# Output projection with seven k-tiles held, and the MLP's first two blocks split by token tile

## The chip, the core and the metric

The kernel runs on one core of one Trainium2 chip. The metric is the device time of one execution in microseconds (us): the median of three runs of the kernel before is 450.49 us (450.48 to 450.57). Names of engines: PE is TensorE's matmul, PEld its weight load, DVE is VectorE, ACT is ScalarE, POOL is GpSimd, SP is SyncE, which issues the loads here.

## What is computed

One layer of a hybrid decoder on 256 tokens of 1024 features, in float32. A token mixer of three gated branches (a short convolution, block-sparse attention, cross-attention into 256 memory tokens) gives `merged`; then

```
x = x + rmsnorm(merged @ w_out, g_post_mix)          # output projection, norm, residual
h = rmsnorm(x, g_pre_ffn)                            # second norm
u = causal_dwconv(h @ w_up, ffn_conv_w, ffn_conv_b)  # 1024 -> 2 x 2816, width 3 over tokens
a, g = split(u)
f = (gelu(a) * g) @ w_down                           # 2816 -> 1024
x = x + rmsnorm(f, g_post_ffn)
```

A norm needs the mean square of a whole row of 1024 features, so nothing of a token's row can be scaled before the last of its columns is there. The change lies in the first three of these lines.

## The kernel before

**Precision.** Each float32 operand is split into two parts, high and low (`hilo`, L265 to L269, for activations; `split_until`, L216 on ACT for `wh` and L217 on DVE for `wl`, for weights), and a product is three matmuls: high by high, high by low, low by high. Where a block of 128 output features is made for all 256 tokens (`mm_wide`, L242 and L244), eight matmuls of 512 columns take both parts of the activations at once and eight of 256 columns add the weights' low parts; ACT and DVE then add the two halves up (L249, L250).

**Weights.** They come from HBM in one stream, in the order of their use: loads of 1 MB, each of two pieces of 128x1024, into three `raw` buffers (L191, issued by SP). A piece is split into a pair from a pool of five (`PARTS`), or into a place lent by a tile that is no longer needed (`extra`): before the change three pieces of w_up go into the places `A`, `A` and `E`. A load can start when DVE has split the earlier content of its buffer; a split into the pool can start when PE has finished with the piece five places back. `weights()` hands the next piece out and splits `ahead` pieces more; with `hold` the piece handed out before is not given back yet.

**Output projection.** Tokens are two tiles of 128 (t = 0 and 1); the 1024 features that are summed over are eight k-tiles. `po[t]` is a pair of PSUM banks of 512 columns each. `down_tile` (L256) runs a k-tile for a token tile as six matmuls of 512 columns: three products by two banks. The first three k-tiles run for both tiles; the last five are held, so that tile 0 can be ended first (its last two k-tiles bank by bank) while tile 1 still has work. The loop is in the hands of a scheduler, which puts the instructions of each engine in an order by its own estimates; pieces of tile 1 can so come between those of tile 0.

**Norms and the second tile** (`residual`, written as a fixed order). `post_norm` takes the mean square on ACT (L279, one instruction for each bank), the factor on three small POOL instructions (L282 to L284), the gain and the residual on DVE (L664, L667). For tile 0 a second mean square follows, and `xs` (L706) is the scaled row. PE turns `xs` into columns (`turn`, L312, eight 128x128 transposes into `tp`). Tile 1's matmuls run meanwhile. Then tile 1's norm, eight transposes of its unscaled `x1`, and ACT (L714) and DVE (L716) make the two parts of `h2T`, eight pieces of 128x256 that hold both tiles. The factor of tile 1's second norm is applied later, after the up projection.

**MLP, first blocks.** `both_blocks` runs the first two blocks of 128 features of w_up side by side: 32 matmuls of 256 columns on the high part of `h2T` (L374, L375), then 16 on its low part (L378). From then on blocks follow one another (`mm_wide`) to the end, with the down projection (`pf`, L256) between them.

Of the kernel before, what the change touches and what calls it, by code (L numbers as in the profile page):

```python
# [12 lines left out]
F32R = mybir.dt.float32r  # L13
BF16 = mybir.dt.bfloat16
AF = mybir.ActivationFunctionType
ALU = mybir.AluOpType
# [84 lines left out]
def trunk(ctx, tc, x, mem, memT_in, weights_in, par_in, rel_bias, g_post_mix, g_post_ffn, buckets, out):  # L101
# [11 lines left out]
    def f32(ap):  # L113
        return ap.bitcast(F32)
# [44 lines left out]
    used, freed = 0, 0  # L159
    extra = dict(zip(range(first_up, first_up + 3), ("A", "A", "E")))  # L160
    extra_tiles = {}
# [3 lines left out]
    def part_tiles(i):  # L165
        if i not in extra:
            return [wp.tile([P, 1024], F32R, tag=tag, name=tag, bufs=PARTS) for tag in ("wh", "wl")]
        tag = extra[i]
        if tag not in extra_tiles:
            extra_tiles[tag] = [sb.tile([P, 2 if tag == "E" else 4, 1024], F32R, tag=tag, name="wx"), 0]  # L170
        t, n = extra_tiles[tag]
        extra_tiles[tag][1] += 2
        return [t[:, n], t[:, n + 1]]
# [193 lines left out]

    def both_blocks(a):

        ws = [weights(hold=i > 0) for i in range(2)]  # L370
        d = acc("ft")
        for k in range(KT):
            for i, (wh, wl) in enumerate(ws):
                nc.tensor.matmul(d[i][:, :S], wh[:, k], a[:, 0, k], start=(k == 0), stop=False)  # L374
                nc.tensor.matmul(d[i][:, :S], wl[:, k], a[:, 0, k], start=False, stop=False)  # L375
        for i, (wh, _) in enumerate(ws):
            for k in range(KT):
                nc.tensor.matmul(d[i][:, S:], wh[:, k], a[:, 1, k], start=False, stop=(k == KT - 1))  # L378
        return d

# [301 lines left out]

    for k in range(KT):
        w = weights(hold=k > KT - 5)
        if k < KT - 5:
            for t in range(NT):
                down_tile(po[t], [parts_of(mg, k, k, t, w)], KT)
        else:
            held.append((k, w))
            if k < KT - 2:  # L690
                down_tile(po[0], [parts_of(mg, k, k, 0, w)], KT)
    down_tile(po[0], [parts_of(mg, k, k, 0, w) for k, w in held[3:]], KT, True)
    split_until(first_up + 3)
    x1 = sb.tile([P, NT, D], F32, tag="qm", name="x1")
    h2T = parts_tile(KT, "B", "h2T")
    r2, dg2, r2s = [], [], []

    def residual():
        post_norm(po[0], x_sb[:, 0], gains[:, 0], x1[:, 0], "ro")
        r2.append(rstd_full(x1[:, 0], "r2"))  # L700
        down_tile(po[1], [parts_of(mg, k, k, 1, w) for k, w in held[:3]], KT)
        down_tile(po[1], [parts_of(mg, k, k, 1, w) for k, w in held[3:]], KT, True)
        banks = [bank("tp") for _ in range(KT // 2)]
        tps = [two(banks[k // 2])[:, k % 2] for k in range(KT)]
        xs = wk.tile([P, 1, D], F32, tag="pT", name="xs", bufs=2)
        nc.vector.tensor_scalar_mul(xs[:, 0], x1[:, 0], r2[0])  # L706
        for k in range(KT):
            turn(tps[k], xs, 0, k)
        post_norm(po[1], x_sb[:, 1], gains[:, 0], x1[:, 1], "ro", (0, 256, 512, D))
        for k in range(KT):  # L710
            turn(tps[k], x1, 1, k)
        for k in range(0, KT, 2):
            for j in (k, k + 1):
                nc.scalar.activation(h2T[:, 0, j], tps[j], AF.Copy, scale=gf[:, j:j + 1])  # L714
            for j in (k, k + 1):
                nc.vector.scalar_tensor_tensor(h2T[:, 1, j], tps[j], gf[:, j:j + 1], f32(h2T[:, 0, j]), op0=ALU.mult,  # L716
                                               op1=ALU.subtract)
        r2.append(rstd_full(x1[:, 1], "r2"))
# [5 lines left out]
    def up(c, f, b0):  # L724
# [23 lines left out]
        for half in (1, 0):  # L748
            u = wk.tile([P, 2 * S], F32, tag="y", name="u", bufs=YB)[:, :n * S]
            res.append(u)  # L750
            if c == 0 and half:
                late.append((half, u, both_blocks(h2T)))
                continue
# [99 lines left out]
```

## Time and profile before

| what | before |
| --- | --- |
| median of three runs | 450.49 us |
| the profiled execution, own time | 449.86 us |
| its span, first to last instruction | 448.1 us |
| PE busy, share of the span | 97% |
| DVE, ACT busy | 80%, 65% |
| output projection on PE | 231.9 to 254.0 us |
| first two MLP blocks on PE | 257.8 to 263.6 us |
| DMA queues, mean | 186 GB/s |

The profile is of one execution; its own time is 0.63 us under the median. Times below are us from the start of its span. The list of instructions in order of time shows, for each engine, when an instruction started, how long it took, and in brackets how long the engine had been idle before it and what ended that. Matmuls are pipelined: one that takes 0.39 us is followed by the next 0.23 us after it started, so a row "x6" has its first start and the end of its sixth.

### The profile page before, as it was taken

To read this page: it belongs to the slowest core of one execution; us is meant where nothing else is said; L and a number is where in the kernel's file an instruction comes from. 1 tells how busy PE (TensorE), PEld (TensorE's weight loads), DVE (VectorE), ACT (ScalarE), POOL (GpSimd) and SP (SyncE) were. 2 spreads that over 40 slices of the span, in tenths; PEclk is the share of its full clock that TensorE was granted. 3 is DMA by queue.
4 is the path that set the end of the run, shared out by engine and by line. 5 is a ranking of instruction groups with operands and counts; after the bars stand their busy time and mean duration, and the time that the engine had idled before them with its cause. 6 is when DMAs were issued, how large, how long until landed. Compare 5 with 4: busy or idle time off the path is not lost.

```text
span 448.1 us, 6694 instructions
## 1 busy us (share of the span) xinstructions
PE 435.7 (97%) x2425; PEld 375.7 (84%) x2425; DVE 358.2 (80%) x635; ACT 292.4 (65%) x533; POOL 15.6 (3%) x40
## 2 busy tenths in 40 slices
PE   7999999999999999999999899999999999999993
PEld 4797888888888998888888698888888888888882
DVE  4687789969987788698777579997878878788875
ACT  5984776756687776675655468866657657657642
POOL 0212000000000000000000300000000000000001
PEclk9999999999999999999999999999999999999998
DMA  7994765534535443555767036555556546546102
GB/s 241 411 407 178 245 225 187 187 114 171 187 105 190 176 144 140 187 177 195 249 225 279 5 140 236 189 187 191 193 182 198 189 176 203 189 176 209 70 1 94
DMA packets 14828, 83.45 MB, mean 186 GB/s; under 512 B 1827, under 2 KB 2636, under 8 KB 6092
## 3 DMA queue, kind: packets, MB, share of 16 engines
q1 hardware_dynamic: 14060, 80.92, 50.9%
q10 hardware_dynamic: 432, 1.05, 0.8%
q0 software_dynamic: 304, 1.06, 0.7%
q8 instruction: 19, 0.31, 0.3%
q14 instruction: 13, 0.11, 0.1%
HBM read 81.96 MB, written 1.06 MB: 185 GB/s over the span
## 4 chain that ended last, share of the span: by engine, by line
PE 91%; ACT 2%; DVE 1%; issue 1%; POOL 0%; POOLq 0%; DVEq 0%; ACTq 0%
PE ft L242 42%; PE ft L244 21%; PE pf L256 13%; PE po L256 5%; PE pv L256 2%; PE po L261 1%; ACT wh L216 1%; ACT junk L279 1%; PE at L261 1%; PE tp L312 0%; PE ft L233 0%; PE ft L378 0%; PE ft L234 0%; PE ft L374 0%; PE ft L235 0%
## 5 line engine op out<-in xcount | busy, mean ns | idle before, releaser
L216 ACT ACTIVATE wh<-raw 128x1024 fp32r<-128x1024 f32 (+1 forms) x139 | 143.1, 1033 | 104.3 <-PE ft L242 66.8
L217 DVE TENSOR_TENSOR wl<-raw,wh 128x1024 fp32r<-128x1024 f32 (+1 forms) x139 | 165.2, 1192 | 55.6 <-ACT wh L216 53.0
L242 PE MATMUL ft<-hT,wh 128*128 128x512 f32 x384 | 97.2, 393 | 0.0
L242 PE MATMUL ft<-h2T,wh 128*128 128x512 f32 x328 | 82.2, 392 | 0.0
L242 PEld LDWEIGHTS ft<-hT,wh 128*128 128x128 f32 x384 | 69.0, 189 | 12.2
L242 PEld LDWEIGHTS ft<-h2T,wh 128*128 128x128 f32 x328 | 59.5, 189 | 11.0
L244 PEld LDWEIGHTS ft<-hT,wl 128*128 128x128 f32 x384 | 52.2, 190 | 3.6
L244 PE MATMUL ft<-hT,wl 128*128 128x256 f32 x384 | 53.6, 282 | 0.0
L249 ACT ACTIVATE t<-ft 128x256 f32<-128x256 f32 x116 | 43.0, 372 | 10.4 <-PE ft L244 10.3
L256 PE MATMUL pf<-wh,f 128*128 128x512 f32 x176 | 49.2, 390 | 0.0
L244 PEld LDWEIGHTS ft<-h2T,wl 128*128 128x128 f32 x328 | 44.9, 190 | 3.3
L244 PE MATMUL ft<-h2T,wl 128*128 128x256 f32 x328 | 45.9, 282 | 0.0
L256 PEld LDWEIGHTS pf<-wh,f 128*128 128x128 f32 x176 | 32.4, 188 | 6.2
L250 DVE TENSOR_TENSOR y<-ft,t 128x256 f32<-128x256 f32 x68 | 28.2, 418 | 2.9 <-ACT t L249 2.6
L256 PE MATMUL pf<-wl,f 128*128 128x512 f32 x88 | 27.5, 390 | 0.0
L745 ACT ACTIVATE u<-v,par 128x256 f32<-128x256 f32 x44 | 24.0, 589 | 3.8 <-DVE v L739 3.7
L594 DVE SCALAR_TENSOR_TENSOR u<-v,par,u 128x255 f32<-128x255 f32 x44 | 19.7, 477 | 0.7 <-ACT u L745 0.7
L595 DVE SCALAR_TENSOR_TENSOR u<-v,par,u 128x254 f32<-128x254 f32 x44 | 19.6, 476 | 0.1
L256 PEld LDWEIGHTS pf<-wl,f 128*128 128x128 f32 x88 | 16.5, 188 | 3.5
L250 DVE TENSOR_TENSOR v<-ft,t 128x256 f32<-128x256 f32 x44 | 17.9, 417 | 0.5 <-ACT t L249 0.5
L256 PE MATMUL po<-wh,mg 128*128 128x512 f32 x64 | 17.9, 389 | 0.0
L282 POOL TENSOR_SCALAR se<-ss 128x1 f32<-128x1 f32 x10 | 3.4, 344 | 404.7 <-ACT junk L279 404.6
(172 smaller groups left out, 549.3 us busy)
## 6 DMA issues: line engine op xcount, KB each, us to landing
raw<-in_weights_dram SPq DMA_DIRECT2D x66, 1024.0 KB, 4.8
raw<-in_weights_dram SPq DMA_DIRECT2D x8, 256.0 KB, 5.7
rawx<-in_weights_dram SPq DMA_DIRECT2D x4, 512.0 KB, 10.2
rawx<-in_weights_dram SPq DMA_DIRECT2D x2, 1024.0 KB, 9.7
raw<-in_weights_dram SPq DMA_DIRECT2D x2, 512.0 KB, 6.9
m_sb<-in_mem_dram SPq DMA_DIRECT2D x2, 512.0 KB, 7.4
x_sb<-in_x_dram SPq DMA_DIRECT2D x2, 512.0 KB, 9.6
bias<-bd POOLq DMA_DIRECT2D x1, 1024.0 KB, 6.1
```

The lines of the kernel that those rows point to most:

```text
L216: nc.scalar.activation(hi, v, AF.Copy)
L217: nc.vector.tensor_tensor(lo, v, f32(hi), ALU.subtract)
L242: nc.tensor.matmul(p, wh[:, k], a[:, :, k], start=(k == 0), stop=False)
L244: nc.tensor.matmul(p[:, :S], wl[:, k], a[:, 0, k], start=False, stop=(k == kt - 1))
L249: nc.scalar.activation(t, p[:, S:], AF.Copy)
L250: nc.vector.tensor_tensor(dst, p[:, :S], t, ALU.add)
L256: nc.tensor.matmul(d, a, w[:, c:c + 512], start=(first and w is wh and a is ah), stop=(last and a is al))
L261: nc.tensor.matmul(dst, a[i], b[j], start=(first and n == 0), stop=(last and n == 2))
L279: nc.scalar.activation(junk, src, AF.Square, scale=D ** -0.5, accum_out=q)
L594: nc.vector.scalar_tensor_tensor(t[:, 1:], src[:, :S - 1], w1, t[:, 1:], op0=ALU.mult, op1=ALU.add)
L595: nc.vector.scalar_tensor_tensor(t[:, 2:], src[:, :S - 2], w0, t[:, 2:], op0=ALU.mult, op1=ALU.add)
L745: nc.scalar.activation(d, v[:, i], AF.Identity, bias=bb, scale=w2)
```

## The change

Four things.

1. Of the output projection's eight k-tiles seven are held (k = 1 to 7) in place of five, and only k = 0 runs for both tiles in the loop. The two last k-tiles' weights get places of their own (`G` and `mk`), and w_up gets a fourth one (`bias`), so six pieces of weights are now in lent places. The loop is written inside a fixed order for PE; `residual` has such an order too, and between the two the scheduler still places the instructions.
2. In `residual`, tile 1's k-tiles 1 to 5 stand ahead of tile 0's transposes and its k-tiles 6 and 7 behind them, bank by bank.
3. The parts of `h2T` are made tile by tile (`spread_out`): sixteen pieces of 128x128 on each of ACT and DVE in place of eight of 128x256.
4. `both_blocks` is gone. `wide_of` runs the first two blocks for one token tile: for each k-tile and block one matmul that takes the high and the low part side by side (2x128 columns), 16 for a tile. Tile 0's stand behind tile 1's last k-tiles and ahead of tile 1's transposes, tile 1's behind its `h2T`. `low_of` then adds the weights' low parts for both tiles (16 matmuls of 256 columns).

The number of matmul columns is the same: 48 matmuls of 256 columns for the two blocks, 96 of 512 for the projection.

```diff
--- before.py
+++ after.py
@@ -157,7 +157,7 @@
     RAWS, PARTS, AHEAD = 3, 5, 3
     raws, parts = [], []
     used, freed = 0, 0
-    extra = dict(zip(range(first_up, first_up + 3), ("A", "A", "E")))
+    extra = dict(zip(range(first_up - 2, first_up + 4), ("G", "mk", "A", "A", "E", "bias")))
     extra_tiles = {}
     lent = {3: ("C", 0), 4: ("C", 1), 5: ("qm", 0), 6: ("cT", 0)}
     lent_tiles = {}
@@ -167,7 +167,7 @@
             return [wp.tile([P, 1024], F32R, tag=tag, name=tag, bufs=PARTS) for tag in ("wh", "wl")]
         tag = extra[i]
         if tag not in extra_tiles:
-            extra_tiles[tag] = [sb.tile([P, 2 if tag == "E" else 4, 1024], F32R, tag=tag, name="wx"), 0]
+            extra_tiles[tag] = [sb.tile([P, 4 if tag == "A" else 2, 1024], F32R, tag=tag, name="wx"), 0]
         t, n = extra_tiles[tag]
         extra_tiles[tag][1] += 2
         return [t[:, n], t[:, n + 1]]
@@ -365,18 +365,17 @@
                 evac(b - 1, y)
             yield
 
-    def both_blocks(a):
-
-        ws = [weights(hold=i > 0) for i in range(2)]
-        d = acc("ft")
+    def wide_of(d, ws, a, t):
+
         for k in range(KT):
-            for i, (wh, wl) in enumerate(ws):
-                nc.tensor.matmul(d[i][:, :S], wh[:, k], a[:, 0, k], start=(k == 0), stop=False)
-                nc.tensor.matmul(d[i][:, :S], wl[:, k], a[:, 0, k], start=False, stop=False)
-        for i, (wh, _) in enumerate(ws):
+            for p, (wh, _) in zip(d, ws):
+                nc.tensor.matmul(two(p)[:, :, tok(t)], wh[:, k], a[:, :, k, tok(t)], start=(t == 0 and k == 0),
+                                 stop=False)
+
+    def low_of(d, ws, a):
+        for p, (_, wl) in zip(d, ws):
             for k in range(KT):
-                nc.tensor.matmul(d[i][:, S:], wh[:, k], a[:, 1, k], start=False, stop=(k == KT - 1))
-        return d
+                nc.tensor.matmul(p[:, :S], wl[:, k], a[:, 0, k], start=False, stop=(k == KT - 1))
 
     def run(gen):
         for _ in gen:
@@ -680,41 +679,51 @@
     def parts_of(a, k, j, t, w):
         return (k, a[:, 0, j, tok(t)], a[:, 1, j, tok(t)], w[0][:, 0], w[1][:, 0])
 
-    for k in range(KT):
-        w = weights(hold=k > KT - 5)
-        if k < KT - 5:
-            for t in range(NT):
-                down_tile(po[t], [parts_of(mg, k, k, t, w)], KT)
-        else:
-            held.append((k, w))
-            if k < KT - 2:
-                down_tile(po[0], [parts_of(mg, k, k, 0, w)], KT)
-    down_tile(po[0], [parts_of(mg, k, k, 0, w) for k, w in held[3:]], KT, True)
-    split_until(first_up + 3)
+    with tc.manual_schedule(engines={mybir.EngineType.PE}):
+        for k in range(KT):
+            w = weights(hold=k > 1)
+            if k < 1:
+                for t in range(NT):
+                    down_tile(po[t], [parts_of(mg, k, k, t, w)], KT)
+            else:
+                held.append((k, w))
+                if k < KT - 2:
+                    down_tile(po[0], [parts_of(mg, k, k, 0, w)], KT)
+        down_tile(po[0], [parts_of(mg, k, k, 0, w) for k, w in held[-2:]], KT, True)
+    split_until(first_up + 4)
     x1 = sb.tile([P, NT, D], F32, tag="qm", name="x1")
     h2T = parts_tile(KT, "B", "h2T")
-    r2, dg2, r2s = [], [], []
+    r2, dg2, r2s, first = [], [], [], []
 
     def residual():
         post_norm(po[0], x_sb[:, 0], gains[:, 0], x1[:, 0], "ro")
         r2.append(rstd_full(x1[:, 0], "r2"))
-        down_tile(po[1], [parts_of(mg, k, k, 1, w) for k, w in held[:3]], KT)
-        down_tile(po[1], [parts_of(mg, k, k, 1, w) for k, w in held[3:]], KT, True)
+        down_tile(po[1], [parts_of(mg, k, k, 1, w) for k, w in held[:-2]], KT)
         banks = [bank("tp") for _ in range(KT // 2)]
         tps = [two(banks[k // 2])[:, k % 2] for k in range(KT)]
         xs = wk.tile([P, 1, D], F32, tag="pT", name="xs", bufs=2)
         nc.vector.tensor_scalar_mul(xs[:, 0], x1[:, 0], r2[0])
-        for k in range(KT):
-            turn(tps[k], xs, 0, k)
+
+        def spread_out(src, t):
+            for k in range(KT):
+                turn(tps[k], src, t, k)
+            for k in range(0, KT, 2):
+                for j in (k, k + 1):
+                    nc.scalar.activation(h2T[:, 0, j, tok(t)], tps[j][:, tok(t)], AF.Copy, scale=gf[:, j:j + 1])
+                for j in (k, k + 1):
+                    nc.vector.scalar_tensor_tensor(h2T[:, 1, j, tok(t)], tps[j][:, tok(t)], gf[:, j:j + 1],
+                                                   f32(h2T[:, 0, j, tok(t)]), op0=ALU.mult, op1=ALU.subtract)
+
+        spread_out(xs, 0)
+        down_tile(po[1], [parts_of(mg, k, k, 1, w) for k, w in held[-2:]], KT, True)
+        ws = [weights(ahead=0) for _ in range(2)]
+        d = acc("ft")
+        wide_of(d, ws, h2T, 0)
         post_norm(po[1], x_sb[:, 1], gains[:, 0], x1[:, 1], "ro", (0, 256, 512, D))
-        for k in range(KT):
-            turn(tps[k], x1, 1, k)
-        for k in range(0, KT, 2):
-            for j in (k, k + 1):
-                nc.scalar.activation(h2T[:, 0, j], tps[j], AF.Copy, scale=gf[:, j:j + 1])
-            for j in (k, k + 1):
-                nc.vector.scalar_tensor_tensor(h2T[:, 1, j], tps[j], gf[:, j:j + 1], f32(h2T[:, 0, j]), op0=ALU.mult,
-                                               op1=ALU.subtract)
+        spread_out(x1, 1)
+        wide_of(d, ws, h2T, 1)
+        low_of(d, ws, h2T)
+        first.append(d)
         r2.append(rstd_full(x1[:, 1], "r2"))
         dg = wk.tile([P, NT, P], F32, tag="dg", name="dg", bufs=1)[:, 0]
         nc.vector.tensor_scalar_mul(dg, ident, r2[1])
@@ -749,7 +758,7 @@
             u = wk.tile([P, 2 * S], F32, tag="y", name="u", bufs=YB)[:, :n * S]
             res.append(u)
             if c == 0 and half:
-                late.append((half, u, both_blocks(h2T)))
+                late.append((half, u, first[0]))
                 continue
             ps_, w = [], None
             for i in range(n):
```

**PE, end of the projection.** In the rows po_2649 and po_2650 are tile 0's two banks, po_2651 and po_2652 tile 1's; `wx` is a piece of weights in a lent place. Before, the last rows of the projection and the transposes of tile 0 (`xs`) and tile 1 (`x`):

```order
L256 MATMUL po_2651<-wh,mg 128x512
L256 MATMUL po_2651<-wl,mg 128x512
L256 MATMUL po_2651<-wh,mg 128x512 x2
L256 MATMUL po_2651<-wl,mg 128x512
L256 MATMUL po_2651<-wh,mg 128x512
L256 MATMUL po_2652<-wh,mg 128x512
L256 MATMUL po_2652<-wl,mg 128x512
L256 MATMUL po_2652<-wh,mg 128x512 x2
L256 MATMUL po_2652<-wl,mg 128x512
L256 MATMUL po_2652<-wh,mg 128x512
L312 MATMUL tp<-ident,xs 128x128 x8
L312 MATMUL tp<-ident,x_2755 128x128 x8
```

Now, at the same place:

```order
L256 MATMUL po_2651<-wh,mg 128x512
L256 MATMUL po_2652<-wh,mg 128x512
L256 MATMUL po_2651<-wl,mg 128x512
L256 MATMUL po_2652<-wl,mg 128x512
L256 MATMUL po_2649<-wx,mg 128x512 x4
L256 MATMUL po_2650<-wx,mg 128x512 x6
L256 MATMUL po_2651<-wh,mg 128x512
L256 MATMUL po_2652<-wh,mg 128x512
L312 MATMUL tp<-ident,xs 128x128 x8
L256 MATMUL po_2651<-wx,mg 128x512 x6
L256 MATMUL po_2652<-wx,mg 128x512 x6
L372 MATMUL ft_2852<-h2T,wx 128x2x128
```

Before, tile 0's last matmul stood as the 71st of 96 (ahead of these rows) and 25 matmuls of tile 1 behind it. Now tile 0's k-tiles 6 and 7 (`po_2649<-wx x4`, `po_2650<-wx x6`) come as the 73rd to 82nd, two matmuls of tile 1 stand between the last of them and the transposes of `xs`, and twelve behind the transposes; tile 1's k-tiles 1 to 5 stand between those of tile 0.

**ACT, the splits ahead of the norm.** `wh` and `wx` are pieces of weights, `t` an addition of the last gates and branches, `mg` the high part of the last two k-tiles of `merged`, `junk` a mean square. Before:

```order
L249 ACTIVATE t<-ft 128x256 x2
L612 ACTIVATE y<-y,bgh 128x256
L216 ACTIVATE wh<-raw 128x1024
L249 ACTIVATE t<-ft 128x256
L216 ACTIVATE wh<-raw 128x1024
L216 ACTIVATE wx<-raw 128x1024 x2
L265 ACTIVATE mg<-y 128x512
L216 ACTIVATE wh<-raw 128x1024 x2
L216 ACTIVATE wx<-raw 128x1024
L279 ACTIVATE junk,ss<-po_2649 128x512
```

Now:

```order
L249 ACTIVATE t<-ft 128x256
L216 ACTIVATE wx<-raw 128x1024 x2
L249 ACTIVATE t<-ft 128x256
L611 ACTIVATE y<-y,bgh 128x256
L216 ACTIVATE wh<-raw 128x1024
L249 ACTIVATE t<-ft 128x256
L216 ACTIVATE wh<-raw 128x1024
L216 ACTIVATE wx<-raw 128x1024 x4
L265 ACTIVATE mg<-y 128x512
L279 ACTIVATE junk,ss<-po_2649 128x512
```

The splits of w_out's k-tiles 6 and 7 stand earlier (first `wx x2`), and four pieces of w_up in place of two stand ahead of `mg`; on DVE the low parts and `mg` are in the same order.

**DVE, the norms and the parts of h2T.** `yo` is the row with its gain, `x` the residual sum. Before:

```order
L706 TENSOR_SCALAR xs<-x_2755,r_2784 128x1024
L664 TENSOR_TENSOR yo<-po_2651,gains 128x512
L664 TENSOR_TENSOR yo<-po_2652,gains 128x512
L667 SCALAR_TENSOR_TENSOR x_2755<-yo,ro,x_sb 128x256 x2
L667 SCALAR_TENSOR_TENSOR x_2755<-yo,ro,x_sb 128x512
L716 SCALAR_TENSOR_TENSOR h2T<-tp,par,h2T 128x256 x8
L720 TENSOR_SCALAR dg<-ident,r_2882 128x128
```

Now:

```order
L705 TENSOR_SCALAR xs<-x_2747,r_2776 128x1024
L714 SCALAR_TENSOR_TENSOR h2T<-tp,par,h2T 128x128 x8
L663 TENSOR_TENSOR yo<-po_2651,gains 128x512
L663 TENSOR_TENSOR yo<-po_2652,gains 128x512
L666 SCALAR_TENSOR_TENSOR x_2747<-yo,ro,x_sb 128x256 x2
L666 SCALAR_TENSOR_TENSOR x_2747<-yo,ro,x_sb 128x512
L714 SCALAR_TENSOR_TENSOR h2T<-tp,par,h2T 128x128 x8
L729 TENSOR_SCALAR dg<-ident,r_2952 128x128
```

Tile 0's pieces of `h2T` now stand ahead of tile 1's norm, tile 1's behind it.

## Rows read from the trace of the kernel before

**Rows 1.** The page, part 1: busy us, share of the span, instructions of each engine.

```profile
PE 435.7 (97%) x2425; PEld 375.7 (84%) x2425; DVE 358.2 (80%) x635; ACT 292.4 (65%) x533; POOL 15.6 (3%) x40
```

**Rows 2.** List of waits: engine, tile, line, releaser, us in total, times, longest.

```profile
PE tp L312 <- DVE x L667: 0.9, 2, 0.7
...
PE tp L312 <- DVE xs L706: 0.6, 1, 0.6
```

**Rows 3.** Instructions in time, PE, projection: start, us, engine, line, operation, count.

```profile
232.02 0.63 PE L256 MATMUL po<-wh,mg 128*128 128x512 f32 x2
...
243.84 1.52 PE L256 MATMUL po<-wh,mg 128*128 128x512 f32 x6
...
247.92 1.07 PE L256 MATMUL po<-wh,mg 128*128 128x512 f32 x4
...
253.58 0.39 PE L256 MATMUL po<-wh,mg 128*128 128x512 f32 x1
```

**Rows 4.** The same list, tile 0's norm: second mean square, then its transposes.

```profile
248.61 0.60 ACT L279 ACTIVATE junk<-po 128x512 bf16<-128x512 f32 x1
...
254.57 1.06 PE L312 MATMUL tp<-ident,xs 128*128 128x128 f32 x8 [0.60 <-DVE xs L706]
```

**Rows 5.** The same list, tile 1's norm, the parts of h2T, first blocks.

```profile
254.09 0.60 ACT L279 ACTIVATE junk<-po 128x512 bf16<-128x512 f32 x1 [0.67 <-PE po L256]
...
256.34 0.83 PE L312 MATMUL tp<-ident,x 128*128 128x128 f32 x4 [0.71 <-DVE x L667]
...
256.81 3.03 ACT L714 ACTIVATE h2T<-tp,par 128x256 fp32r<-128x256 f32 x8 [2.04 <-PE tp L312]
...
257.40 0.66 PE L312 MATMUL tp<-ident,x 128*128 128x128 f32 x4 [0.23 <-DVE x L667]
257.69 3.23 DVE L716 SCALAR_TENSOR_TENSOR h2T<-tp,par,h2T 128x256 fp32r<-128x256 f32 x8 [0.35 <-ACT h2T L714]
...
257.81 0.36 PE L374 MATMUL ft<-h2T,wx 128*128 128x256 f32 x1
...
261.72 2.08 PE L378 MATMUL ft<-h2T,wx 128*128 128x256 f32 x16
...
263.64 2.00 PE L242 MATMUL ft<-h2T,wx 128*128 128x512 f32 x8
```

**Rows 6.** Groups by shape, DVE reading PSUM: busy us, mean ns, idle before.

```profile
L539 DVE CUSTOM_DVE_ANT_0 e<-sc,bias 128x256 f32<-128x256 f32 x8 | 3.4, 419 | 0.0
...
L539 DVE CUSTOM_DVE_ANT_0 e<-sc,bias 128x128 f32<-128x128 f32 x8 | 2.2, 279 | 0.0
```

**Rows 7.** Load of k-tiles 6, 7 (SP); landing; splits and `mg` on ACT, DVE.

```profile
225.70 0.33 SPq L191 DMA_DIRECT2D raw<-in_weights_dram  x1
...
DMA to landing us min/median/max: 4.7/4.7/5.0
...
235.94 1.99 ACT L216 ACTIVATE wx<-raw 128x1024 fp32r<-128x1024 f32 x2
...
237.21 2.35 DVE L217 TENSOR_TENSOR wx<-raw,wx 128x1024 fp32r<-128x1024 f32 x2
237.83 0.62 ACT L265 ACTIVATE mg<-y 128x512 fp32r<-128x512 f32 x1
239.48 0.68 DVE L269 SCALAR_TENSOR_TENSOR mg<-y,mg 128x512 fp32r<-128x512 f32 x1
```

**Rows 8.** PE at both ends of the span; stretches with PEclk (third from right).

```profile
0.77 4.00 PE L418 MATMUL pw<-const-bfloat16-1.0 128*128 128x512 bf16 x9 [0.77 <-PEq L842]
...
7.03 0.63 PE L256 MATMUL pmv<-wh,memT 128*128 128x512 f32 x2
...
440.84 0.39 PE L256 MATMUL pf<-wh,f 128*128 128x512 f32 x1
...
444.50:445.00 0.50, 0.00 (x0) 0.00 (x0) 0.10 (x1) 0.00 (x0) 0.00 (x0) 1.00 0.72 234
445.00:445.50 0.50, 0.00 (x0) 0.00 (x0) 0.00 (x0) 0.00 (x0) 0.00 (x0) 0.55 1.04 372
```

## The prediction

> **What bounds the kernel now.** I read the page's first part, then the list of waits, then the instructions in order of time around the change. The page has PE busy for 97% of the span [rows 1], so time can be won only where PE stands idle, and lost wherever it newly does. The waits show PE idle at two places of this stretch: for `xs`, 0.6 us, and for tile 1's `x`, 0.9 us in two waits [rows 2]. I count PE's idle time here as what its spacing leaves over. Matmuls of 512 columns follow one another every 0.2265 us ((253.58 - 243.84) / 43 steps) [rows 3], those of 256 columns every 0.12 us ((263.64 - 261.72) / 16), transposes every 0.10 us ((257.81 - 257.40) / 4) [rows 5]. From the start of the last projection matmul, 253.58, to the first full block at 263.64 are 10.06 us; the work in it is 0.23 + 16 x 0.10 + 48 x 0.12 = 7.59 us, so PE is idle for about 2.5 us. That is all that the change could win here.
>
> **The change part by part.** The matmul columns stay the same, so I look for PE's new idle time, from the order of the rows.
>
> *Tile 0's end.* Tile 0's last matmul was the 71st of 96 and started at 247.92; now it is the 82nd, 11 steps later: 247.92 + 11 x 0.2265 = 250.41, if nothing ahead of it waits (below). Holding seven k-tiles was to end tile 0 sooner, but the order has tile 1's k-tiles 1 to 5 between those of tile 0.
>
> *Tile 0's norm.* From the last matmul's start the mean square begins 0.51 us later (253.58 to 254.09) [rows 3, 5], and from the second mean square to the transposes are 5.96 us (248.61 to 254.57) [rows 4]. None of that chain is changed: ACT, DVE and POOL have the same instructions in it. So 6.47 us from the last matmul to the transposes; before, it was 6.65, since the second mean square queued behind the first, which now starts six matmuls ahead. The transposes of `xs` can start at 250.41 + 6.47 = 256.88.
>
> *What PE has meanwhile.* Before, 25 matmuls of tile 1 (5.7 us) covered this chain but for 0.6 us [rows 2]. Now two stand there. PE is free at 250.41 + 3 x 0.2265 = 251.09 and takes its instructions in their order: tile 1's twelve others stand behind the transposes. New idle time: 256.88 - 251.09 = 5.8 us. This is the large term.
>
> *Tile 1.* Transposes until 256.88 + 8 x 0.10 = 257.68, then twelve matmuls, the last starting at 257.68 + 11 x 0.2265 = 260.17. From tile 1's last matmul to its first transposes were 2.76 us (253.58 to 256.34) [rows 3, 5]: now 262.93. This wait was all idle before, apart from the transposes of `xs`; now tile 0's 16 matmuls of `wide_of` (1.9 us) lie in it, from 260.40 to 262.32. That is what the change saves: PE waits 0.6 us there. Tile 0's pieces of `h2T` (eight on ACT, eight on DVE) start at about 257.4 and end by 260 to 261, under the twelve matmuls; they now stand ahead of tile 1's mean square and gain, and could push tile 1's norm by up to 0.4 us, which I put into the range.
>
> *h2T of tile 1.* Before, the first matmuls on `h2T` needed only high parts and started 1.47 us after the first transposes (256.34 to 257.81), running at their own pace while DVE made the low parts [rows 5]. `wide_of` takes high and low side by side, so it goes at DVE's pace. ACT began 0.47 us after the first transposes (256.34 to 256.81), DVE another 0.88 us later, after two pieces of ACT [rows 5]. The trace has no such piece of 128x128. One of 128x256 takes 3.23 / 8 = 0.40 us [rows 5]; another DVE operation from PSUM loses 0.14 us with half the columns (419 to 279 ns) [rows 6], so I take 0.27 us, eight in 2.15 us. The ends are no gain at all (3.23 us) and half (1.6 us). ACT's two pieces I put at 0.7. DVE's last low part: 262.93 + 0.47 + 0.7 + 2.15 = 266.25. Behind it stand two matmuls of `wide_of` and 16 of `low_of`, 18 x 0.12 = 2.16 us: the next block starts at 268.4, where it started at 263.64 before: **+4.8 us**. The ends of DVE's piece give +4.2 and, with the 0.4 us from above, +6.2.
>
> *Does anything ahead of tile 0's end wait?* Its k-tiles 6 and 7 need `mg`, whose high part now stands behind four splits of w_up. The load of k-tiles 6 and 7 is issued at 225.70 and lands 4.7 us later [rows 7], 230.4; their splits on ACT (1.0 us each) and DVE (1.2 each) free the buffer at about 233.9; the load of w_up's third and fourth pieces then lands at 238.6. Two splits and `mg` on ACT: 238.6 + 1.99 + 0.62 = 241.2. On DVE, whose splits of the first two w_up pieces end at about 240.9: + 2.35 + 0.68 = 243.9 [rows 7]. PE wants the high part at its 60th matmul, 243.84 + 7 x 0.2265 = 245.4, the low part at the 73rd, 248.4. So 4 us to spare; I cost it at nothing. The extra place for weights costs nothing either: it fills earlier what is used later, and the next piece from the pool is wanted one block (2.8 us) later than before.
>
> *After the stretch* the instructions of the MLP are the same on PE, which is busy to the end, so the shift stays.
>
> **The clock.** An idle stretch of 5.8 us has no like in this trace outside its end. There PE's last matmul starts at 440.84, and PEclk is 1.00 until 445.0 and 0.55 in the half microsecond behind: it falls to 0.50, the 1.2 GHz level, about 3.8 us after PE's end (440.84 + 0.39 = 441.23) [rows 8]. At the front nine matmuls of 512 columns take 4.00 us, 0.44 each, the pace of 1.2 GHz (512 / 1.2 GHz = 0.43 us); the two at 7.03 take 0.63 together, 0.24 apart if one is 0.39, that of 2.4 GHz [rows 3, 8]. So after an idle stretch like the new one the rows make a fall likely, and PE would then work at half pace for 4.0 to 6.3 us, losing half of that, 2.0 to 3.1 us. The work there (transposes and tile 1's twelve matmuls, 3.5 us at full pace) leads straight to tile 1's norm, so the loss counts. I take 2.2 us, near the lower end, because the front's upper bound holds 1.2 us without matmuls.
>
> The Trainium skill has the same rule, and it speaks against this change: the page "TensorE: Matmul & The Clock Gate", section "Part 1: The HAM clock gate (the "warmup" mystery)", says that the idle array goes back to 1.2 GHz and gets 2.4 GHz back only after a busy spell. By that rule the sum is the one with the fall; the rows of the span's end agree with it, and no row before shows a fall between matmuls.
>
> **The rivals.**
> - *A, stall with a fall of the clock:* 450.49 + 4.8 + 2.2 = 457.5 us, with its ends 456.7 (4.2 + 2.0) to 459.8 (6.2 + 3.1). For it: 5.8 us idle against 3.8 us at the end of the span. Chance 0.60.
> - *B, stall without a fall:* 455.3 us, 454.7 to 456.7. For it: one fall alone is in the trace, and its delay may differ from one execution to the next. Chance 0.27.
> - *C, the data come late as well:* if the load of w_up's third and fourth pieces, or a split ahead of `mg`, is over 4 us later than worked out, tile 0 ends later by the rest. The scheduler's order, which puts tile 1's k-tiles ahead, is what one would write for late data. At 3 us beyond the spare time: 460.5 us. Against it: loads land in 4.7 to 5.0 us throughout this stretch [rows 7]. Chance 0.06.
> - *D, faster:* tile 1's held matmuls do cover tile 0's norm. It needs the order that the change describes to be the one that runs: each tile 1 matmul between tile 0's last and the transposes takes 0.2265 us off the idle time; from 21 of them on (4.8 / 0.2265) the change wins, and with 26 the idle 5.8 us is gone and 450.49 + 4.8 - 5.8 = 449.5 us is left. Against it: two stand there. Chance 0.04.
> - *E, no difference:* about twenty of them, or a norm chain that is shorter by 5 us. Nothing shows it. Chance 0.03.
>
> **How the numbers follow.** The likeliest is A, 457.5 us. The sum is made on the profiled execution (449.86 us, 0.63 under the median); all of it lies inside the span, so the difference is added to the median, 450.49. The range takes in A and B with their ends, 454.5 to 459.8; C, D and E lie outside, 0.13 together. Within 0.2% (0.9 us, about what a measurement of this kernel can tell from no change) I put E: faster 0.04, same 0.03, slower 0.93.
>
> **What would show it.** In the profile after, PE should wait for `xs` (L705, ended by DVE) for 5 to 6 us from about 251.1, once, where it waited 0.6 us; the transposes of `xs` should start near 256.9, tile 1's near 263 (265 with the slow clock), the block at L242 near 268.4 (270.6). PEclk should be under 1.00 for some microseconds around 255 to 261, or else B holds. The wait between tile 1's end and its transposes should have shrunk to about 0.6 us, and the first matmuls behind them should wait for DVE's L714. If `xs` is ready by 252, or if tile 0's last matmul starts near 248 or before, the first step is wrong; if PE waits ahead of that for `mg` or `wx`, C was at work; if PE is idle in the MLP behind, my claim that the shift simply stays is wrong.

## The result, and the profile after

The changed kernel takes 457.02 us (median of four runs, 456.63 to 457.57) against 450.49 us (450.40 to 450.57, four runs) for the kernel before: a ratio of 1.0152, interval 1.014 to 1.0164. It is slower by 1.5%. The predicted time was 457.5 us.

Page of the kernel after, head and parts 1 and 2 (span; busy us, share, instructions; busy tenths in 40 slices):

```profile
span 454.9 us, 6714 instructions
...
PE 437.9 (96%) x2425; PEld 377.6 (83%) x2425; DVE 358.9 (79%) x643; ACT 293.4 (65%) x541; POOL 15.0 (3%) x40
...
PE   7999999999999999999999599999999999999993
...
PEclk9999999999999999999999699999999999999998
```

PE has the same 2425 instructions as in [rows 1], in a span that is 6.8 us longer (454.9 against 448.1). Both new things are in slice 23 (slices of 11.4 us): PE was busy for half of it, and the granted clock was low. Waits of the kernel after (us in total, times, longest):

```profile
PE tp L312 <- DVE xs L705: 5.6, 1, 5.6
...
PE tp L312 <- DVE x L666: 0.7, 2, 0.5
```

They answer to [rows 2]: the wait for `xs` has gone from 0.6 to 5.6 us, the one for tile 1's `x` from 0.9 to 0.7. Instructions in time of the kernel after, PE in this stretch (start, us, engine, line, operation, tile, count, idle before):

```profile
248.31 2.43 PE L256 MATMUL po<-wx,mg 128*128 128x512 f32 x10
250.57 0.61 PE L256 MATMUL po<-wh,mg 128*128 128x512 f32 x2
256.79 1.94 PE L312 MATMUL tp<-ident,xs 128*128 128x128 f32 x8 [5.60 <-DVE xs L705]
258.38 3.99 PE L256 MATMUL po<-wx,mg 128*128 128x512 f32 x12
262.21 2.07 PE L372 MATMUL ft<-h2T,wx 128*128 128x256 f32 x16
264.74 0.83 PE L312 MATMUL tp<-ident,x 128*128 128x128 f32 x4 [0.46 <-DVE x L666]
...
268.52 2.08 PE L378 MATMUL ft<-h2T,wx 128*128 128x256 f32 x16
270.43 2.00 PE L242 MATMUL ft<-h2T,wx 128*128 128x512 f32 x8
```

Two matmuls of tile 1 stand behind tile 0's last one, and then PE stands still. The eight transposes of `xs` took 1.94 us, where they took 1.06 before [rows 4], and the twelve matmuls behind them 3.99 us, where twelve at full pace take 2.99 (e1_fill below): this is the slow clock. The block at L242 starts 6.8 us later than in [rows 5], which is the whole difference of the spans. Stretches of one us of the kernel after (busy PE, PEld, DVE, ACT, POOL; granted clock third from right):

```profile
253.00:254.00 1.00, 0.00 (x0) 0.00 (x0) 0.96 (x2) 0.61 (x2) 0.00 (x0) 0.85 0.00 0
254.00:255.00 1.00, 0.00 (x0) 0.00 (x0) 0.00 (x0) 0.84 (x4) 0.22 (x1) 0.50 0.00 0
...
260.00:261.00 1.00, 1.00 (x5) 0.81 (x4) 0.31 (x2) 0.00 (x0) 0.00 (x0) 0.74 0.00 0
261.00:262.00 1.00, 1.00 (x7) 0.79 (x6) 0.16 (x1) 0.69 (x2) 0.10 (x1) 1.00 0.00 0
```

The clock went to 1.2 GHz at about 253.7 (0.85 is full speed for 0.7 of that us and half speed for the rest), 2.5 us after PE's end at 250.57 + 0.61 = 251.18. It came back at about 260.5, 3.7 us after PE took up work at 256.79.

### The profile page after: what moved, and what is told of

It is laid out like the page before. It is cut to its first block, busy times and chain, and to the rows that moved or that the text cites. A ratio compares the mean times of both kernels' runs of the same rounds, so it can differ in the third digit from the quotient of the medians.

```text
span 454.9 us, 6714 instructions
## 1 busy us (share of the span) xinstructions
PE 437.9 (96%) x2425; PEld 377.6 (83%) x2425; DVE 358.9 (79%) x643; ACT 293.4 (65%) x541; POOL 15.0 (3%) x40
## 3 DMA queue, kind: packets, MB, share of 16 engines
q0 software_dynamic: 304, 1.06, 0.7%
HBM read 81.96 MB, written 1.06 MB: 183 GB/s over the span
## 4 chain that ended last, share of the span: by engine, by line
PE 90%; ACT 2%; DVE 1%; issue 1%; POOL 1%; POOLq 0%; DVEq 0%; ACTq 0%
PE ft L242 41%; PE ft L244 21%; PE pf L256 13%; PE po L256 5%; PE pv L256 2%; PE po L261 1%; ACT junk L279 1%; PE tp L312 1%; ACT wh L216 1%; PE at L261 1%; DVE x L666 1%; PE ft L372 0%; PE ft L233 0%; PE ft L234 0%; PE ft L235 0%
## 5 line engine op out<-in xcount | busy, mean ns | idle before, releaser
L216 ACT ACTIVATE wh<-raw 128x1024 fp32r<-128x1024 f32 (+1 forms) x136 | 140.0, 1033 | 101.2 <-PE ft L242 66.8
L217 DVE TENSOR_TENSOR wl<-raw,wh 128x1024 fp32r<-128x1024 f32 (+1 forms) x136 | 161.7, 1191 | 53.2 <-ACT wh L216 51.2
L242 PE MATMUL ft<-hT,wh 128*128 128x512 f32 x384 | 97.2, 393 | 0.0
L242 PE MATMUL ft<-h2T,wh 128*128 128x512 f32 x320 | 80.1, 392 | 0.0
L242 PEld LDWEIGHTS ft<-hT,wh 128*128 128x128 f32 x384 | 69.0, 189 | 12.3
L242 PEld LDWEIGHTS ft<-h2T,wh 128*128 128x128 f32 x320 | 58.1, 189 | 10.7
L244 PEld LDWEIGHTS ft<-h2T,wl 128*128 128x128 f32 x320 | 43.8, 190 | 3.2
L244 PE MATMUL ft<-h2T,wl 128*128 128x256 f32 x320 | 44.8, 282 | 0.0
L256 PE MATMUL po<-wh,mg 128*128 128x512 f32 x48 | 13.2, 389 | 0.0
```

Source lines behind the costliest of these rows:

```text
L216: nc.scalar.activation(hi, v, AF.Copy)
L217: nc.vector.tensor_tensor(lo, v, f32(hi), ALU.subtract)
L242: nc.tensor.matmul(p, wh[:, k], a[:, :, k], start=(k == 0), stop=False)
L244: nc.tensor.matmul(p[:, :S], wl[:, k], a[:, 0, k], start=False, stop=(k == kt - 1))
L256: nc.tensor.matmul(d, a, w[:, c:c + 512], start=(first and w is wh and a is ah), stop=(last and a is al))
```

## The experiments

My theory: the time is set by how many matmuls of tile 1 are left to stand between tile 0's last one and the transposes of `xs`, and the idle PE then loses its clock as well. The change holds seven k-tiles, but its loop and its `residual` are two separate fixed orders, and what comes between them sends 28 of the 30 held matmuls out ahead of tile 0's end. The rivals are in the expectations.

**e1_fill: the idle stretch filled, its length left as it is.**

```diff
         xs = wk.tile([P, 1, D], F32, tag="pT", name="xs", bufs=2)
+        one = nc.const_aps.tensor(1.0, (P, 512), BF16)
+        for _ in range(24):
+            nc.tensor.matmul(banks[3], one[:, :P], one, start=True, stop=True)
         nc.vector.tensor_scalar_mul(xs[:, 0], x1[:, 0], r2[0])
```

> The changed kernel with 24 matmuls of 512 constant bf16 columns (5.1 us at 2.4 GHz) put on PE between tile 1's first 30 matmuls and the transposes of xs, into a bank that the transposes then fill; nothing waits for them. It takes away the idle stretch for the clock but not the wait for xs. Theory (PE's wait for xs costs 4.8 us, the clock's fall behind it about 1.9 us more, half of the 3.7 us that PE worked at 1.2 GHz): PEclk stays at 1.00, the transposes still start near 256.8 us, and the time is 457.0 - 1.9 = 455.1 us. Rival (the lower clock costs nothing, since PE waits for DVE behind it anyway): 457.0 us.

Measured: 455.03 us (454.98 to 455.56; the kernel before, measured beside it, 450.29), ratio 1.0111, interval 1.0095 to 1.0126. PE in time, and the granted clock over two stretches of 6 us of e1_fill (the trace has records of 23 of the 24 added matmuls):

```profile
251.21 5.42 PE L707 MATMUL tp<-const-bfloat16-1.0 128*128 128x512 bf16 x23
256.95 1.06 PE L312 MATMUL tp<-ident,xs 128*128 128x128 f32 x8 [0.32 <-DVE xs L708]
257.77 2.99 PE L256 MATMUL po<-wx,mg 128*128 128x512 f32 x12
```

```profile
250.00:256.00 6.00, 5.94 (x28) 2.99 (x28) 2.80 (x4) 2.41 (x8) 1.94 (x6) 1.00 0.00 0
256.00:262.00 6.00, 5.68 (x35) 4.68 (x34) 4.00 (x11) 3.50 (x12) 0.44 (x4) 1.00 0.00 0
```

The wait is still there, hidden under work that belongs to nothing (`xs` came at 256.95 against 256.79), but the clock stays full: the transposes take 1.06 us instead of 1.94, the twelve matmuls 2.99 instead of 3.99. Against its own kernel before it loses 4.74 us, the changed kernel 6.53: 1.8 us of the loss are the clock, and 4.7 are left for the stall, net of what the rest of the change saves (e5_both).

**e5_both: the early blocks undone, the held k-tiles left.** `h2T` of both tiles is written at once behind tile 1's norm, and the first two blocks run over both tiles together, as before.

```diff
...
-        spread_out(xs, 0)
+        for k in range(KT):
+            turn(tps[k], xs, 0, k)
...
-        wide_of(d, ws, h2T, 0)
-        post_norm(po[1], x_sb[:, 1], gains[:, 0], x1[:, 1], "ro", (0, 256, 512, D))
-        spread_out(x1, 1)
-        wide_of(d, ws, h2T, 1)
-        low_of(d, ws, h2T)
+        for k in range(KT):
+            for i, (wh, wl) in enumerate(ws):
+                nc.tensor.matmul(d[i][:, :S], wh[:, k], h2T[:, 0, k], start=(k == 0), stop=False)
+                nc.tensor.matmul(d[i][:, :S], wl[:, k], h2T[:, 0, k], start=False, stop=False)
...
```

> The changed kernel with its third and fourth parts undone: h2T made for both tiles at once behind tile 1's norm, and the first two blocks run as before the change (32 matmuls on the high parts, 16 on the low). The projection's order, with the wait for xs, stays. Theory (wide_of saves by filling the wait between tile 1's end and its transposes): the first full block starts 7.3 us after tile 1's first transposes, as before the change, where the changed kernel has 5.7: 457.0 + 1.6 = 458.6 us. Rival (the smaller parts and matmuls that wait for DVE cost time): 455.5 us or less.

Measured: 458.71 us (458.34 to 460.26), ratio 1.0196, interval 1.018 to 1.0211. PE in time of e5_both:

```profile
257.54 1.94 PE L312 MATMUL tp<-ident,xs 128*128 128x128 f32 x8 [5.58 <-DVE xs L705]
259.13 3.70 PE L256 MATMUL po<-wx,mg 128*128 128x512 f32 x12
265.20 0.83 PE L312 MATMUL tp<-ident,x 128*128 128x128 f32 x4 [2.36 <-DVE x L666]
...
272.50 2.00 PE L242 MATMUL ft<-h2T,wx 128*128 128x512 f32 x8
```

The wait for `xs` is the same 5.6 us, so the early blocks are not what costs. Without them the wait for tile 1's `x` is 2.4 us instead of 0.5, 1.9 us more. Not all of that reaches the end: from these transposes to the block at L242 are 272.50 - 265.20 = 7.30 us, in the changed kernel 270.43 - 264.74 = 5.69. So the early blocks are worth 1.6 us in the changed kernel, hidden behind the larger loss. The medians differ by 1.7 us, but not at the same clock: it fell later here (257.2) and was low for 3.1 us of PE's work.

**e2_cover: the loop and `residual` in one fixed order**, so that 30 held matmuls stand behind tile 0's last one.

```diff
-    with tc.manual_schedule(engines={mybir.EngineType.PE}):
+    def project():
         for k in range(KT):
...
-    split_until(first_up + 4)
...
+        project()
+        split_until(first_up + 4)
         residual()
```

> The changed kernel with the projection's loop and all that follows up to the first hidden block in one fixed order, so that tile 0's 48 matmuls end as the 54th and tile 1's 30 matmuls of k-tiles 1 to 5 stand between them and the transposes of xs. Seven k-tiles held, lent places, wide_of and the parts tile by tile stay. Theory (the place of tile 1's matmuls is what makes the wait): the 5.6 us wait for xs shrinks to 1 or 2 us and the clock stays at 1.00. ACT has two splits of w_up ahead of tile 0's mean square, whose load lands at about 244.4 us, so the norm starts near 246.4 and the transposes near 253.2: 1.2 us later than before at the first full block, 451.7 us (450.5 to 453). Rival (the held weights, their early splits and the fourth lent place are what costs): 456 to 457 us.

Measured: 450.02 us (449.58 to 450.44), ratio 0.9996, interval 0.9987 to 1.0005: the loss is gone. The wait for `xs` is no longer in the list. PE and ACT in time of e2_cover:

```profile
243.04 2.56 PE L256 MATMUL po<-wx,mg 128*128 128x512 f32 x10 [0.30 <-DVE mg L269]
...
252.25 1.03 PE L312 MATMUL tp<-ident,xs 128*128 128x128 f32 x8
```

```profile
242.48 2.01 ACT L216 ACTIVATE wx<-raw 128x1024 fp32r<-128x1024 f32 x2 [1.58 <-DMA raw<-in_weights_dram]
244.39 0.57 ACT L279 ACTIVATE junk<-po 128x512 bf16<-128x512 f32 x1
```

It came out 1.7 us below my 451.7, and below the 450.5 at the range's lower end. I had the last load of w_up that stands ahead of tile 0's mean square land at 244.4; ACT took it up at 242.48, so the mean square began at 244.39 and not at 246.4, and the 30 matmuls covered the norm after all. Two things were left that I took for costs: ACT's splits of that load stand ahead of the mean square, and PE waits 0.3 us for `mg`. The trace bears out the second alone: tile 0's second mean square waited 0.65 us for PE, not for a split, and the transposes of `xs` waited for nothing.

**e4_order: the same order, with `mg` and the splits put where nobody waits for them.** The last part of `mg` is made before the splits of k-tiles 6 and 7; the third split of w_up stands behind tile 0's residual, the fourth behind `xs`. The edit against e2_cover (the first cut takes that part of `mg` out of its old place and keeps the loop from splitting pieces of w_up):

```diff
...
+                if k == 2:
+                    hilo(mg[:, 0, 6:8], mg[:, 1, 6:8], merged[3, 0], 0.5)
...
         post_norm(po[0], x_sb[:, 0], gains[:, 0], x1[:, 0], "ro")
+        split_until(first_up + 3)
...
         nc.vector.tensor_scalar_mul(xs[:, 0], x1[:, 0], r2[0])
+        split_until(first_up + 4)
...
-        split_until(first_up + 4)
+        split_until(first_up + 2)
```

> As e2_cover, and the order on ACT and DVE mended: the last merged parts (mg) ahead of the splits of k-tiles 6 and 7, w_up's third piece split after tile 0's residual, the fourth after xs, in the gaps of tile 0's norm. Theory: tile 0's last matmul starts at 244.1 us, xs is ready at 250.5, PE's cover ends at 251.1, so no wait for xs; tile 1's last matmul at 254.4, its transposes at 257.1, the first full block 5.7 us later at 262.8, where it started at 263.64 before: 450.49 - 0.8 = 449.7 us. Rival (wide_of and the sixteen smaller parts cost more than they save, whatever the order): 451 us or more.

Measured: 449.36 us (449.07 to 449.83, 11 runs), ratio 0.998, interval 0.9971 to 0.9989: faster than both kernels, but only by 0.2% against the one before. Measured once more, on another chip:

> e4_order once more, on whichever chip this call gets: if its lead is the order's and not that chip's, about 449.3 us, 0.9 below the kernel before; rival: no difference from the kernel before, 450.2.

Measured: 449.42 us (448.95 to 449.74, 11 runs) against 450.11, ratio 0.9983, interval 0.9974 to 0.9992. PE in time of e4_order, then of e9_order_again:

```profile
232.39 0.63 PE L256 MATMUL po<-wh,mg 128*128 128x512 f32 x2
...
241.94 2.88 PE L256 MATMUL po<-wx,mg 128*128 128x512 f32 x12
...
251.47 1.03 PE L312 MATMUL tp<-ident,xs 128*128 128x128 f32 x8
252.25 2.98 PE L256 MATMUL po<-wx,mg 128*128 128x512 f32 x12
...
263.29 2.00 PE L242 MATMUL ft<-h2T,wx 128*128 128x512 f32 x8
```

```profile
232.10 0.63 PE L256 MATMUL po<-wh,mg 128*128 128x512 f32 x2
...
263.01 2.00 PE L242 MATMUL ft<-h2T,wx 128*128 128x512 f32 x8
```

The chain from tile 0's last matmul, 241.94 + 11 x 0.2265 = 244.43, to the transposes of `xs` is now covered. Executions reach the projection at moments some tenths of a us apart, so I count from its first matmul to the block at L242: 263.29 - 232.39 = 30.90 us in e4_order and 263.01 - 232.10 = 30.91 in e9_order_again, against 263.64 - 232.02 = 31.62 before [rows 3, 5]. These 0.7 us are the lead that the medians show (0.93 and 0.69). Against e2_cover (264.08 - 232.58 = 31.50) e4_order gains 0.6 us. Tile 0's last twelve matmuls take that much longer in e2_cover, with the wait for `mg` among them (245.44 - 242.12 = 3.32 us, here 244.66 - 241.94 = 2.72); that the moved splits gave any of it is not shown, since both were changed at once.

**e6: a dose of uncovered matmuls.** In e4_order two, three or four of the held k-tiles are put ahead of tile 0's last two, so that 18, 12 or 6 matmuls are left behind instead of 30. The work is the same. For 18:

```diff
+        down_tile(po[1], [parts_of(mg, k, k, 1, w) for k, w in held[:2]], KT)
         down_tile(po[0], [parts_of(mg, k, k, 0, w) for k, w in held[-2:]], KT, True)
...
-        down_tile(po[1], [parts_of(mg, k, k, 1, w) for k, w in held[:-2]], KT)
+        down_tile(po[1], [parts_of(mg, k, k, 1, w) for k, w in held[2:-2]], KT)
```

> e4_order with two of tile 1's seven held k-tiles (12 matmuls) put ahead of tile 0's last two k-tiles, so that 18 instead of 30 are left to stand between tile 0's last matmul and the transposes of xs. The work is the same. My theory (what counts is how many matmuls are left behind tile 0's last one): tile 0's norm starts 12 x 0.2265 = 2.7 us later, e4_order had about 0.5 us to spare, so TensorE waits about 2.2 us for xs and the time is 449.4 + 2.2 = 451.6 us, at a full clock, since in the other traces the clock fell no sooner than 2.5 us after the last matmul. Rival (the idle time is made up for later, or other things in the new order made e4_order fast): no more than 450.

> As e6_behind18, with three k-tiles (18 matmuls) ahead and 12 left behind tile 0's last one. My theory: a wait for xs of 18 x 0.2265 - 0.5 = 3.6 us and 449.4 + 3.6 = 453.0 us; if the clock falls in an idle stretch of this length, up to 2 us more, 455. Rival: no more than 450.

> As e6_behind18, with four k-tiles (24 matmuls) ahead and 6 left behind tile 0's last one. My theory: a wait for xs of 24 x 0.2265 - 0.5 = 4.9 us and 449.4 + 4.9 = 454.3 us at a full clock, 456.3 with the fall of the clock that the changed kernel showed. Rival: no more than 450.

Measured (the kernel before beside them: 450.10):

| left behind | expected wait | wait in the trace | expected time | measured |
| --- | --- | --- | --- | --- |
| 18 | 2.2 | 2.2 | 451.6 | 453.61 (453.23 to 453.81) |
| 12 | 3.6 | 3.6 | 453.0, to 455 | 453.9 (453.0 to 456.1) |
| 6 | 4.9 | 4.9 | 454.3, to 456.3 | 456.4 (456.31 to 456.75) |

PE in time of e6_behind18, of e6_behind12 and of e6_behind6, three fences in this order:

```profile
253.82 1.15 PE L312 MATMUL tp<-ident,xs 128*128 128x128 f32 x8 [2.22 <-DVE xs L710]
254.64 4.59 PE L256 MATMUL po<-wx,mg 128*128 128x512 f32 x12
```

```profile
254.93 1.07 PE L312 MATMUL tp<-ident,xs 128*128 128x128 f32 x8 [3.58 <-DVE xs L710]
255.75 3.03 PE L256 MATMUL po<-wx,mg 128*128 128x512 f32 x12
```

```profile
256.95 1.94 PE L312 MATMUL tp<-ident,xs 128*128 128x128 f32 x8 [4.93 <-DVE xs L710]
258.54 3.53 PE L256 MATMUL po<-wx,mg 128*128 128x512 f32 x12
```

The waits fall on the line that the theory draws, 0.2265 us for each matmul moved. The times do so only with the clock added, and there I was wrong for 18: I had expected no fall in so short a stretch. After 2.2 us of idleness its twelve matmuls took 4.59 us; after 3.6 us, in e6_behind12, they took 3.03, at full pace. Granted clock of e6_behind18:

```profile
253.00:254.00 1.00, 0.18 (x2) 0.21 (x3) 1.00 (x2) 0.00 (x0) 0.00 (x0) 1.00 0.00 0
254.00:255.00 1.00, 1.00 (x9) 1.00 (x8) 0.88 (x2) 0.74 (x3) 0.00 (x0) 0.83 0.00 0
...
257.00:258.00 1.00, 1.00 (x4) 0.80 (x3) 0.08 (x1) 0.35 (x1) 0.00 (x0) 0.50 1.00 426
258.00:259.00 1.00, 1.00 (x5) 0.81 (x5) 0.63 (x1) 0.34 (x2) 0.22 (x1) 0.96 0.74 311
```

The clock fell at about 254.7, when PE had been at work again for 0.8 us. Of e6_behind12 the profiled execution (453.08 us) shows 1.00 from 250 to 263; its other runs were 453.0, 454.71 and 456.1 us. A fall could explain 454.71, but 456.1 is 3 us more than the profiled one, and no fall seen here cost that much. There is no trace of these two, and their mean granted clocks (0.994 and 0.990, against 0.992 of both shorter ones) do not tell: the cause of the spread is open.

**e8_fill18: eight matmuls of constants in the 2.2 us of e6_behind18.**

```diff
+        one = nc.const_aps.tensor(1.0, (P, 512), BF16)
+        for _ in range(8):
+            nc.tensor.matmul(banks[3], one[:, :P], one, start=True, stop=True)
         xs = wk.tile([P, 1, D], F32, tag="pT", name="xs", bufs=2)
```

> e6_behind18 with 8 matmuls of constants, 128x128 by 128x512 in bf16, put into its 2.2 us wait for xs; they belong to no result. e6_behind18 took 453.61 us, 2.0 more than its wait explains, and its trace shows the clock at 1.2 GHz for 3.7 us although TensorE stood still for no more than 2.2 us. If the 2.0 us are the clock's, then here it stays at 2.4 GHz, the wait shrinks to about 0.4 us and the end comes where the wait alone put it, 451.6 us. Rival (the extra 2 us come from something else in that order, a transfer or a later wait): 453.6.

Measured: 451.67 us (451.56 to 451.86; before 450.11). PE in time of e8_fill18:

```profile
253.78 1.06 PE L312 MATMUL tp<-ident,xs 128*128 128x128 f32 x8 [0.45 <-DVE xs L713]
254.60 3.00 PE L256 MATMUL po<-wx,mg 128*128 128x512 f32 x12
```

`xs` comes at the same time (253.78 against 253.82), so nothing was taken off the chain, and the time is where the wait alone puts it. The 2.0 us that e6_behind18 took beyond its wait are the clock's; 1.65 of them stand in the traces (453.51 against 451.86 us for the profiled executions). The clock was at 1.2 GHz there from 254.7 to 258.1, so for 3.4 us and not the 3.7 of my expectation.

**e7_order_both: e4_order without the early blocks.** The edit is that of e5_both.

> e4_order with its third part undone: the hidden activations of both tiles are written at once, behind the second tile's norm, and the first two blocks of w_up run over both tiles together, as in the kernel before. My theory: the wait for the second tile's x, now uncovered, grows by about 1.6 us, as it did from the changed kernel to e5_both (456.9 - 454.9 = 2.0 us of span there, with another clock), so about 451.0 us: holding k-tiles alone gives nothing over the kernel before, and the early blocks are what gives e4_order its lead. Rival (the early blocks only move the wait): 449.4 us.

Measured: 452.49 us (450.97 to 452.76), ratio 1.0043, interval 1.0028 to 1.0058. PE in time of e7_order_both:

```profile
252.64 2.98 PE L256 MATMUL po<-wx,mg 128*128 128x512 f32 x12
257.99 0.83 PE L312 MATMUL tp<-ident,x 128*128 128x128 f32 x4 [2.37 <-DVE x L667]
...
265.29 2.00 PE L242 MATMUL ft<-h2T,wx 128*128 128x512 f32 x8
```

The sign is right, the median 1.5 us above my figure: without the early blocks the better order gains nothing over the kernel before. The wait for tile 1's `x` grew by 1.9 us, as in e5_both, and from these transposes to L242 are again 7.30 us: 1.6 more than with the early blocks. The profiled execution (451.5 us, span 449.7 against 447.7), at a full clock, shows that and 0.4 us that it had lost before the projection (first matmul at 232.78 against 232.39). Three other runs took 452.5 to 452.8 us. The idle stretch of 2.4 us is of the length at which e6_behind18 lost its clock, and their mean granted clock is 0.991 against 0.995 and 0.994 in the two shorter ones, but that mean differs as much without any cost in time (0.998 in e4_order's trace, 0.993 in e9_order_again's), so the cause of that last us is open.

## Why the prediction was right, point by point

*Tile 0's end and the stall.* Predicted: last matmul at 250.41, transposes at 256.88. In the trace after: 250.57 - 0.23 = 250.34, and 256.79. The norm chain took 6.45 us against 6.47. PE's wait was 5.6 us where 5 to 6 were expected. e1_fill left it and e2_cover took it away; e6 gave its slope.

*Nothing ahead of it waits.* The load of w_up's third and fourth pieces was expected to land at 238.6, `mg` to be ready at 241.2 (high) and 243.9 (low). ACT and DVE in time of the kernel after:

```profile
238.76 2.01 ACT L216 ACTIVATE wx<-raw 128x1024 fp32r<-128x1024 f32 x2 [0.89 <-DMA raw<-in_weights_dram]
240.67 0.61 ACT L265 ACTIVATE mg<-y 128x512 fp32r<-128x512 f32 x1
```

```profile
242.66 0.68 DVE L269 SCALAR_TENSOR_TENSOR mg<-y,mg 128x512 fp32r<-128x512 f32 x1
```

That is 241.28 and 243.34, with PE in want of them from 245.4: rival C is out.

*Tile 1's norm.* From its last matmul (262.21 - 0.23 = 261.98) to its transposes (264.74) are 2.76 us, the value read from before to the hundredth. So the up to 0.4 us that I had kept for tile 0's pieces of `h2T` in front of the norm were not needed, nor were they at full clock (e1_fill: 263.13 - 260.38 = 2.75). The wait there was 0.46 us for the first transposes against 0.6.

*The pieces of 128x128*, of which before had no example (DVE in time, after):

```profile
265.88 2.18 DVE L714 SCALAR_TENSOR_TENSOR h2T<-tp,par,h2T 128x128 fp32r<-128x128 f32 x8
```

They start 1.14 us after the transposes (taken: 0.47 + 0.7) and last 2.18 us (taken: 2.15). The way from the transposes to L242 is 5.69 us against 5.47, the first term that is off, by 0.2.

*The clock.* It was the term with the least to rest on, and the one that is off most. From the transposes of `xs` to tile 1's last matmul are 261.98 - 256.79 = 5.19 us; at full pace they were to be 3.29. So the loss is 1.9 us (1.8 by e1_fill), where I took 2.2 and put the lower end at 2.0: the clock came back 3.7 us after PE's restart, sooner than the 4.0 I read from the front of the span. The Trainium skill's page "TensorE: Matmul & The Clock Gate", section "Part 1: The HAM clock gate (the "warmup" mystery)", says that an array left idle goes back to 1.2 GHz; this trace agrees (2.5 us after PE's end), and e6_behind12's, with 3.6 us idle at full clock, shows that not every such stretch does it.

*The sum.* -0.1 (start of the transposes), -0.3 (clock) and +0.2 (to L242) make 7.0 into 6.8, the difference of the spans. The two larger errors have opposite signs, so that the time came within 0.5 us is in part luck; the stall itself, 5.6 us, was read rightly. The medians differ by 6.53: the profiled execution after was 0.35 us under its median, the one before 0.63. Case A happened; B, without a fall, is what e1_fill made, 455.03 against the 455.3 given for it. D, the held matmuls covering the norm, needed its order to be the one that runs: e2_cover made that order and came to 450.02, and e4_order, with `mg` and the splits moved as well, to 449.36, against 449.5. *After the stretch* the shift stayed: 6.8 us at L242 and at the end.

## What to carry to other kernels

Work that is held back to cover a wait covers it only if it stands behind the instruction that starts the wait; read that in PE's order, count the matmuls between the last producer and the first consumer, and compare their time with the chain. If a fixed order is written in two pieces, what runs between them is not fixed: e2_cover, which makes it one piece, gave back the whole loss of 6.5 us. Then look for what still makes PE wait inside the covered stretch, here the 0.3 us for `mg`: with `mg` and the splits moved, e4_order was 0.7 us faster than e2_cover (449.36 against 450.02).

## What the runs showed of the hardware that I had not expected

Whether PE's clock falls after an idle stretch isn't told by the length of the stretch. It fell after stretches of 2.2 us (e6_behind18), 4.9, 5.6 and 5.6 us, and did not in executed stretches of 2.4 us (e7_order_both) and 3.6 us (e6_behind12). Counted from PE's last matmul, the fall came after 2.5 us in the changed kernel, 3.1 in e6_behind18, 4.2 in e6_behind6 and 5.2 in e5_both, beside the 3.8 at the end of the kernel before [rows 8]; in e6_behind18 PE was at work again by then. Granted clock of e6_behind6, of e5_both, and of e9_order_again near the front of its span:

```profile
256.00:257.00 1.00, 0.05 (x1) 0.08 (x2) 0.95 (x2) 0.00 (x0) 0.01 (x1) 0.61 0.00 0
```

```profile
257.00:258.00 1.00, 0.46 (x3) 0.49 (x4) 0.40 (x1) 0.00 (x0) 0.00 (x0) 0.60 0.00 0
```

```profile
7.00:8.00 1.00, 1.00 (x4) 0.79 (x3) 0.65 (x2) 0.31 (x1) 0.00 (x0) 0.65 1.00 309
```

The last row adds that the kernel alone does not fix the clock's course. e9_order_again is e4_order's kernel. In its trace the clock fell at 7.3 us, behind waits of PE of 1.6 and 0.2 us, and came back at 10.7; in e4_order's trace PE kept the low pace of the span's start (0.43 us for 512 columns) until about 8.5 us, and no fall is shown before the end. The two executions took 449.22 and 449.51 us. In e6_behind12 and e6_behind6 the clock fell at the front as well. What sets the moment was not tried here.

The price of a fall in the stretch of the change was about half of the time that PE then worked at the lower clock. From the transposes of `xs` to L242 it was 1.35 us in e6_behind6 (256.95 to 270.12 are 13.17 us, in e4_order 263.29 - 251.47 = 11.82), with the clock back 2.7 us after PE's restart, and 1.8 us in the changed kernel (270.43 - 256.79 = 13.64), with the clock back after 3.7 us.
